# Rotating q and k in stacks of four tiles, scaling the attention probabilities on ScalarE, and a third w0 low part on GpSimd

## The chip, the cores and the metric

The kernel runs on one core of a Trainium2 chip. The core has five engines that work side by side, each on its own queue of instructions and in the order of that queue: TensorE (PE: matrix products, with weight loads called PEld in the profile), VectorE (DVE), ScalarE (ACT), GpSimd (POOL) and SyncE (SP, which issues most of the DMAs). They meet through semaphores. The metric is the device time of one execution in microseconds (us), here the median of the runs shown.

## The reference, cut to what matters

One layer of an encoder, float32 throughout, 512 positions of 1024 features. The part around the change is the attention branch: q and k are projected, the first 32 of the 128 features of each head are rotated by position, and three groups of four heads attend with a dilation of 1, 4 and 16. The groups are combined by weights from their softmax denominators.

```python
def partial_rope(t):                       # t: (B, S, H, 128)
    half = ROPE_DIM // 2                   # ROPE_DIM = 32
    ...
    x1, x2, rest = tf[..., :half], tf[..., half:ROPE_DIM], tf[..., ROPE_DIM:]
    return concatenate([x1 * cos - x2 * sin, x2 * cos + x1 * sin, rest], axis=-1)

def dilated_window_attention(q, k, v, dilation, radius):
    ...
    s = einsum('bdnqhe,bdnkhe->bdnhqk', qb, kw) * scale
    s = where(valid, s, MASK_VALUE)
    m = max(s, axis=-1, keepdims=True)
    p = exp(s - m)
    denom = sum(p, axis=-1, keepdims=True)
    o = einsum('bdnhqk,bdnkhe->bdnhqe', p, vw) / denom
    ...

def reference(x, ...):
    n = rms_norm(h, norm_mix_pre)
    z_gmlp, q, k, v, gates = split(n @ w_in, split_points)
    y_a = gmlp_spatial_gating(gelu(z_gmlp), ...)
    q, k = partial_rope(q), partial_rope(k)
    for g, (window, dilation) in enumerate(ATTN_PATTERNS):      # (128,1), (512,4), (2048,16)
        o_g, lse_g = dilated_window_attention(q[g], k[g], v[g], dilation, window // (2 * dilation))
    w_mix = softmax(stack(lses), axis=0)
    y_b = sum(w_mix[..., None] * stack(outs), axis=0)
    merged = sigmoid(gate_a) * (y_a @ w_branch_a) + sigmoid(gate_b) * (y_b @ w_branch_b)
    h = h + rms_norm(merged @ w_out, norm_mix_post)
    ...                                                         # and an MLP with relu squared
```

## The kernel before, in words

**Products.** Every large product is made of three matmuls in a one-pass float32 type (F32R): each operand is split into a high part (ScalarE copies it into F32R, `hi`) and a low part (a subtraction, `lo`, mostly on VectorE), and `mm3` (lines 82 to 86) adds high x high, high x low and low x high. So each weight tile of 128 x 1024 that TensorE uses is first split by one ScalarE and one VectorE instruction (`wsplit`, lines 70 to 76). In `nc.tensor.matmul(ps, a, b)` the first operand, a, is the stationary one that a weight load brings into the array, and b is the moving one that is streamed past it.

**The front.** The four blocks of x (in the order 1, 2, 3, 0) are loaded, squared and summed (`square_x`, ScalarE), scaled to `xn` on VectorE, turned by TensorE (line 180) into `pt`, and split into `nh` and `nl` (`norm_x`). Beside this the eight tiles of the first weight, w0, are split (`split_w0`); the low parts of tiles 3 and 7 are made by GpSimd, the other six by VectorE. For each block 24 matmuls give `pv`.

**The v groups 1 and 2** (`token_major`) take as stationary operand every fourth column of nh and nl: `n[:, k, ROT + r:ROT + S:4]`. A later product of the same form (`COL_V`) takes 128 neighbouring columns.

**The heads.** For each h of 4, `project_qk` goes through the groups g = 1, 2, 0; for each it loads the q and k weights, splits them and lets `feature_tile` make `pf` (24 matmuls of 128x512), the 128 features of the head by 512 positions. `rope_tile` then takes it out of PSUM:

```python
nc.vector.stream_shuffle(sw, ps[0:32], ...)                          # L312 swapped halves
nc.scalar.activation(dst, v(ps), AF.Copy)                            # L313
nc.gpsimd.tensor_tensor(sw, sw, rope[:, 1], op=ALU.mult)             # L314 times sin
nc.vector.tensor_tensor(dst[0:32], v(ps[0:32]), v(rope[:, 0]), ...)  # L315 times cos
nc.vector.tensor_tensor(dst[0:32], dst[0:32], v(sw), op=ALU.add)     # L316
```

For the groups 1 and 2, `v` reorders positions (l r) to (r l), so that `q1`, `k1`, `q2` and `k2` lie in SBUF as four runs of 128 neighbouring columns, one for each residue r. `scores_b` multiplies them in plain float32 (line 373, 32 matmuls of 128x128, each two records in the profile) into `psb`; `scores_a` does it for group 0 with split operands into `psa`. `softmax_tile` masks, takes the maximum (VectorE) and the exponential (ScalarE). `mix(h)` combines the groups: a short chain of small steps with two small matmuls, `pp` (line 398) and `pc` (line 421), and at its end VectorE scales the eight probability tiles (lines 427 and 429). `attend(h)` turns the scaled tiles on TensorE (lines 448, 461), splits or copies them (`ptah`, `ptal`, `ptb`) and multiplies with v into `py`; it is emitted while head h + 1 is projected. The attention of the last head is interleaved with the product `pf` of u that follows the product `pv` of `COL_V`.

**What sets the order.** The program is written once in Python; a scheduler then orders each engine's instructions by its own timing model, and the pools add waits wherever a tile's buffer is used again. Two pools matter here. In PSUM `psA`, tag "T" has a single buffer: `pp`, `pc`, the turned tiles `pt` of the heads 0 to 2 and the first `pf` of u take turns in it. Tag "acc" has four. In SBUF the weight halves `hi` and `lo` of `wpool` have three buffers each, so a new split waits until TensorE has used the one three before.

Of the kernel before, what the change touches and what calls it, by code (L numbers as in the profile page):

```python
# [16 lines left out]
P = 128  # L17
# [19 lines left out]
def block_kernel(ctx: ExitStack, tc: tile.TileContext, x, norm_mix_pre, w_in, b_gate, ln_v_gain, ln_v_bias,  # L37
# [151 lines left out]
    def split_w0(k):  # L189
        raw = w0raw[k // 2][:, k % 2]  # L190
        hi = w0pool.tile([P, GW], F32R, name="w0hi")
        lo = w0pool.tile([P, GW], F32R, name="w0lo")
        ins = nc.scalar.activation(hi, raw, AF.Copy)
        (nc.gpsimd if k in (3, 7) else nc.vector).tensor_tensor(lo, raw, hi.bitcast(F32), op=ALU.subtract)
        w0.append((hi, lo))
        return ins
# [111 lines left out]

    def rope_tile(ps, dst, perm):
        v = (lambda a: a.rearrange("p (l r) -> p r l", r=4)) if perm else (lambda a: a)  # L310
        sw = apool.tile([32, S], F32, name="sw", bufs=2)
        nc.vector.stream_shuffle(sw, ps[0:32], [(i + 16) % 32 for i in range(32)])  # L312
        nc.scalar.activation(dst, v(ps), AF.Copy)  # L313
        nc.gpsimd.tensor_tensor(sw, sw, rope[:, 1], op=ALU.mult)  # L314
        nc.vector.tensor_tensor(dst[0:32], v(ps[0:32]), v(rope[:, 0]), op=ALU.mult)  # L315
        nc.vector.tensor_tensor(dst[0:32], dst[0:32], v(sw), op=ALU.add)  # L316

    def project_qk(h):
        got = {}
        for g in (1, 2, 0):  # L320
            if g == 2 and h:
                attend(h - 1)
            hd0 = (g * NH + h) * HD
            raw = wload([2, KD, P], lambda r: [(r[:, 0], fcols(w_in, COL_Q + hd0, KD, P)), (r[:, 1], fcols(w_in, COL_K + hd0, KD, P))], "qkw")
            for j, nm in enumerate("qk"):
                wh, wl = wsplit(raw[:, j])
                ps = feature_tile(wh, wl, KD, nhn, nln)
                if g:
                    d = apool.tile([P, 4, P], F32, name=f"{nm}{g}")
                    rope_tile(ps, d, True)  # L330
                    got[nm, g] = d
                else:
                    t = apool.tile([P, S], F32, name="qk0t", bufs=2)
                    rope_tile(ps, t, False)
                    w = S if nm == "q" else S + P
                    o = 0 if nm == "q" else ROT
                    hi = apool.tile([P, w], F32R, name=f"{nm}0h")
                    lo = apool.tile([P, w], F32R, name=f"{nm}0l")
                    split_into(hi[:, o:o + S], lo[:, o:o + S], t)
                    if nm == "k":  # L340
                        for z, y in ((hi, nc.scalar), (lo, nc.vector)):
                            zf = z.bitcast(F32)
                            for dst, src in ((z[:, 0:ROT], zf[:, S:S + ROT]), (z[:, S + ROT:], zf[:, ROT:2 * ROT])):
                                if y is nc.scalar:
                                    y.activation(dst, src, AF.Copy)
                                else:
                                    y.tensor_copy(dst, src)
                    got[nm, g] = (hi, lo)
            if g == 2:
                scores_b(h, got)  # L350
        scores_a(h, got)

# [39 lines left out]
    def mix(h):  # L392
# [585 lines left out]
def _constants():  # L978
# [3 lines left out]
    cos, sin = np.cos(ang).astype(np.float32).T, np.sin(ang).astype(np.float32).T  # L982
    rope = np.stack([np.concatenate([cos, cos]), np.concatenate([-sin, sin])]).astype(np.float32)
    i = np.arange(P)[:, None]
# [26 lines left out]
```

## Time and profile before

| what | value |
|---|---|
| median of 3 runs | 814.27 us (813.33 to 814.29) |
| the profiled execution | 814.04 us, of which 812.3 us is the span from the first to the last instruction |
| PE busy | 801.9 us, 99% of the span |
| DVE busy | 546.8 us, 67% |
| ACT busy | 371.6 us, 46% |
| POOL busy | 85.4 us, 11% |
| span 88 to 243 us (the heads): busy | PE 155.00, DVE 132.75, ACT 65.44, POOL 41.89 of 155 us |
| span 243 to 290 us (v of the gating, u, last head): busy | PE 47.00, DVE 32.06, ACT 22.11, POOL 15.80 of 47 us |

How to read it: a row of a group names the line, the engine, the operation, output<-inputs, the shape, and after the bar the busy time and the mean duration of one. In a timeline the first number is the start in us from the span's start, the second the time covered; a remark in brackets says how long the engine was idle before it and for what. The durations of matmuls are modelled with their way through the array, so the pace of TensorE is read from the distances of starts, not from durations. In the waits, "A <- B" means that A's engine sat idle until B had ended.

### The profile page before, as it was taken

To read this page: it belongs to the slowest core of one execution; us is meant where nothing else is said; L and a number is where in the kernel's file an instruction comes from. 1 tells how busy PE (TensorE), PEld (TensorE's weight loads), DVE (VectorE), ACT (ScalarE), POOL (GpSimd) and SP (SyncE) were. 2 spreads that over 40 slices of the span, in tenths; PEclk is the share of its full clock that TensorE was granted. 3 is DMA by queue.
4 is the path that set the end of the run, shared out by engine and by line. 5 is a ranking of instruction groups with operands and counts; after the bars stand their busy time and mean duration, and the time that the engine had idled before them with its cause. 6 is when DMAs were issued, how large, how long until landed. Compare 5 with 4: busy or idle time off the path is not lost.

```text
span 812.3 us, 11650 instructions
## 1 busy us (share of the span) xinstructions
PE 801.9 (99%) x4629; PEld 711.8 (88%) x4629; DVE 546.8 (67%) x916; ACT 371.6 (46%) x609; POOL 85.4 (11%) x92
## 2 busy tenths in 40 slices
PE   8999999999999999999999999999999999999996
PEld 5899888888888889999988899999999888888885
DVE  6772788978783978788656579988887533333324
ACT  6342334434344545454535447666676522332212
POOL 2012113232222400000000200000000000000000
PEclk9999999999999999999999999999999999999999
DMA  9367333232131283244446223333334632332202
GB/s 294 123 228 187 98 104 104 53 90 67 52 104 53 65 284 105 79 112 122 130 137 227 103 79 94 114 105 104 106 108 144 235 109 103 104 104 77 79 1 104
DMA packets 83960, 95.34 MB, mean 117 GB/s; under 512 B 2417, under 2 KB 70033, under 8 KB 82882
## 3 DMA queue, kind: packets, MB, share of 16 engines
q1 hardware_dynamic: 80208, 77.60, 31.5%
q0 software_dynamic: 3696, 17.00, 6.0%
q8 instruction: 36, 0.59, 0.3%
q14 instruction: 18, 0.15, 0.1%
q10 hardware_dynamic: 2, 0.00, 0.0%
HBM read 86.20 MB, written 8.39 MB: 116 GB/s over the span
## 4 chain that ended last, share of the span: by engine, by line
PE 94%; DMA 2%; DVE 2%; ACT 1%; SPq 0%; issue 0%; DVEq 0%; POOLq 0%; ACTq 0%
PE pacc L880 12%; PE pd L85 9%; PE pd L84 9%; PE pd L86 9%; PE pf L86 9%; PE pf L85 9%; PE pf L84 9%; PE pgacc L555 6%; PE ptp L880 4%; PE pv L84 4%; PE pv L85 3%; PE pv L86 3%; PE pgS L555 2%; DMA xt<-in_x_dram 1%; PE psb L373 1%; PE py L485 1%
## 5 line engine op out<-in xcount | busy, mean ns | idle before, releaser
L84 PE MATMUL pf<-nh,hi 128*128 128x512 f32 x240 | 94.6, 394 | 0.0
L85 PE MATMUL pf<-nl,hi 128*128 128x512 f32 x240 | 94.5, 394 | 0.0
L86 PE MATMUL pf<-nh,lo 128*128 128x512 f32 x240 | 94.2, 392 | 0.0
L85 PE MATMUL pd<-hl,hh 128*128 128x512 f32 x224 | 87.2, 389 | 0.0
L84 PE MATMUL pd<-hl,hh 128*128 128x512 f32 x224 | 86.2, 389 | 0.0
L86 PE MATMUL pd<-hl 128*128 128x512 f32 x224 | 86.0, 389 | 0.0
L80 DVE TENSOR_TENSOR hl<-hid,hh 128x512 fp32r<-128x512 f32 x28 | 19.2, 693 | 75.6 <-ACT hh L79 75.6
L880 PE MATMUL pacc<-nt,hl 128*128 128x256 f32 x504 | 67.7, 280 | 0.1
L880 PEld LDWEIGHTS pacc<-nt,hl 128*128 128x128 f32 x504 | 62.7, 188 | 0.4 <-ACT hl L79 0.3
L79 ACT ACTIVATE hh<-hid 128x512 fp32r<-128x512 f32 x28 | 17.4, 630 | 89.0 <-PE pd L85 89.0
L314 POOL TENSOR_TENSOR sw<-sw,rope 32x512 f32<-32x512 f32 x24 | 41.9, 1745 | 131.7 <-DVE sw L312 114.6
L86 PEld LDWEIGHTS pf<-nh,lo 128*128 128x128 f32 x240 | 45.1, 188 | 8.9
L84 PEld LDWEIGHTS pf<-nh,hi 128*128 128x128 f32 x240 | 45.1, 188 | 8.7
L85 PEld LDWEIGHTS pf<-nl,hi 128*128 128x128 f32 x240 | 45.1, 188 | 8.6
L86 PEld LDWEIGHTS pd<-hl 128*128 128x128 f32 x224 | 42.0, 188 | 8.8
L84 PEld LDWEIGHTS pd<-hl,hh 128*128 128x128 f32 x224 | 42.0, 188 | 8.7
L85 PEld LDWEIGHTS pd<-hl,hh 128*128 128x128 f32 x224 | 42.0, 188 | 8.5
L80 DVE TENSOR_TENSOR hl<-dnw,hl 128x1024 fp32r<-128x1024 f32 x32 | 39.1, 1225 | 13.9 <-ACT hl L79 13.9
L74 ACT ACTIVATE hi<-qkw 128x1024 fp32r<-128x1024 f32 x24 | 25.4, 1058 | 49.3 <-PE pf L85 25.5
L880 PE MATMUL pacc<-n,hl 128*128 128x256 f32 x336 | 45.2, 280 | 0.4 <-ACT z L905 0.4
L75 DVE TENSOR_TENSOR lo<-qkw,hi 128x1024 fp32r<-128x1024 f32 x24 | 36.9, 1538 | 12.1 <-ACT hi L74 11.5
L79 ACT ACTIVATE hl<-s 128x1024 fp32r<-128x1024 f32 x28 | 29.6, 1058 | 29.1 <-DVE s L864 10.8
(317 smaller groups left out, 1992.3 us busy)
## 6 DMA issues: line engine op xcount, KB each, us to landing
upw<-in_w_up_dram SPq DMA_DIRECT2D x16, 1024.0 KB, 5.5
dnw<-in_w_down_dram SPq DMA_DIRECT2D x16, 1024.0 KB, 4.9
qkw<-in_w_in_dram SPq DMA_DIRECT2D x24, 512.0 KB, 5.3
gw<-in_w_in_dram SPq DMA_DIRECT2D x16, 512.0 KB, 5.4
slab<-in_w_in_dram SPq DMA_DIRECT2D x6, 1024.0 KB, 9.8
sum<-sum POOLq DMA_DIRECT2D x4, 1024.0 KB, 7.8
nt<-sum POOLq DMA_DIRECT2D x4, 1024.0 KB, 8.0
wow<-in_w_out_dram SPq DMA_DIRECT2D x4, 1024.0 KB, 4.8
```

Source lines behind the costliest of these rows:

```text
L74: nc.scalar.activation(hi, raw, AF.Copy)
L75: (sub or nc.vector).tensor_tensor(lo, raw, hi.bitcast(F32), op=ALU.subtract)
L79: nc.scalar.activation(hi, src, AF.Copy)
L80: return nc.vector.tensor_tensor(lo, src, hi.bitcast(F32), op=ALU.subtract)
L84: nc.tensor.matmul(ps, ah, bh, start=start, stop=False)
L85: nc.tensor.matmul(ps, ah, bl, start=False, stop=False)
L86: return nc.tensor.matmul(ps, al, bh, start=False, stop=stop)
L314: nc.gpsimd.tensor_tensor(sw, sw, rope[:, 1], op=ALU.mult)
L373: nc.tensor.matmul(ps[:, rr, g - 1], got["q", g][:, r], got["k", g][:, r], start=True, stop=True)
L485: nc.tensor.matmul(o, v12[:, g, r, hs], ptb[r // 2][:, r % 2, g], start=False, stop=(r == 3 and g == 1), skip_group_check=True)
L555: nc.tensor.matmul(ps, a[:, j], b[:, j], start=first and not (j or i), stop=(j == KH - 1 and i == 2), skip_group_check=True)
L880: nc.tensor.matmul(ps, a[:, j], b[:, j], start=first and not (j or m), stop=(j == KH - 1 and m == 2), skip_group_check=True)
```

## The change

1. In the front, the low part of w0 tile 5 is made by GpSimd too, and the squares of the third and fourth block are emitted after the high part of the second block, not before.
2. `rope_tile` is replaced. ScalarE copies each `pf` out in plain order (`d`) and its first 32 rows once more into 32 rows of a stack `st` of 128 partitions. When q1, k1, q2 and k2 are there, `rotate` shuffles, multiplies and adds the whole stack at once, and ScalarE copies the four results back into the first 32 rows of each tile. q0 and k0 are a second stack of 64 rows. The table `rope` has its 32 rows four times.
3. The reordering is gone from the copies: `got` holds a view, `d.rearrange("p (l r) -> p r l", r=4)`, so `scores_b` reads every fourth column.
4. The eight probability tiles are scaled by ScalarE.

```diff
-        (nc.gpsimd if k in (3, 7) else nc.vector).tensor_tensor(lo, raw, hi.bitcast(F32), op=ALU.subtract)
+        (nc.gpsimd if k in (3, 5, 7) else nc.vector).tensor_tensor(lo, raw, hi.bitcast(F32), op=ALU.subtract)
...
-        with tc.issue_after(ins.ins):
-            rs[2], sq = square_x(blocks[2], xts[2])
...
         if i == 0:
             with tc.issue_after(hi.ins):
-                rs[3], _ = square_x(blocks[3], xts[3])
+                for j in (2, 3):
+                    rs[j], _ = square_x(blocks[j], xts[j])
...
-    rope = apool.tile([32, 2, S], F32, name="rope")
+    rope = apool.tile([P, 2, S], F32, name="rope")
...
+    def rotate(st, tiles):
+        rows = 32 * len(tiles)
+        sw = apool.tile([P, S], F32, name="sw")
+        nc.vector.stream_shuffle(sw[:rows], st[:rows], [(i + 16) % 32 for i in range(32)])
+        nc.gpsimd.tensor_tensor(sw[:rows], sw[:rows], rope[:rows, 1], op=ALU.mult)
+        nc.vector.tensor_tensor(st[:rows], st[:rows], rope[:rows, 0], op=ALU.mult)
+        nc.vector.tensor_tensor(st[:rows], st[:rows], sw[:rows], op=ALU.add)
+        for i, d in enumerate(tiles):
+            nc.scalar.activation(d[0:32], st[32 * i:32 * i + 32], AF.Copy)
...
+            if g != 2:
+                st, tiles = apool.tile([P, S], F32, name="st", bufs=2), []
...
                 ps = feature_tile(wh, wl, KD, nhn, nln)
-                if g:
-                    d = apool.tile([P, 4, P], F32, name=f"{nm}{g}")
-                    rope_tile(ps, d, True)
-                    got[nm, g] = d
...
+                d = apool.tile([P, S], F32, name=f"{nm}{g}")
+                nc.scalar.activation(d, ps, AF.Copy)
+                i = len(tiles)
+                nc.scalar.activation(st[32 * i:32 * i + 32], ps[0:32], AF.Copy)
+                tiles.append(d)
+                got[nm, g] = d.rearrange("p (l r) -> p r l", r=4)
             if g == 2:
+                rotate(st, tiles)
                 scores_b(h, got)
+            elif g == 0:
+                rotate(st, tiles)
...
         for i in range(4):
-            nc.vector.tensor_scalar(probs[h, "b", i], probs[h, "b", i], cf[:, 1, i:i + 1], None, op0=ALU.mult)
+            nc.scalar.activation(probs[h, "b", i], probs[h, "b", i], AF.Copy, scale=cf[:, 1, i:i + 1])
         for i in range(4):
-            nc.vector.tensor_scalar(probs[h, "a", i], probs[h, "a", i], ca[:, i:i + 1], None, op0=ALU.mult)
+            nc.scalar.activation(probs[h, "a", i], probs[h, "a", i], AF.Copy, scale=ca[:, i:i + 1])
```

Lines of the changed kernel are a few numbers higher from `scores_b` on (the score matmul of line 373 stands on line 378, `pp` on 403, `pc` on 426).

The places where the scheduler's new order matters are shown next. First TensorE where the product `pv` of `COL_V` ends and the product `pf` of u begins, with the mix of the last head between them (`pp`, `pc`), in the program before:

```order
L398 MATMUL pp<-xa,perm 128x32
L85 MATMUL pv<-lo,nh 128x512
...
L84 MATMUL pv<-hi,nh 128x512
L85 MATMUL pv<-lo,nh 128x512
L421 MATMUL pc<-xc,perm 128x16
L86 MATMUL pv<-hi,nl 128x512
```

And in the changed program, the same place, with buffer numbers:

```order
L86 MATMUL pv_2210<-hi_2299,nl_80 128x512
L490 MATMUL py_1872<-ptb_1909,v12_89 128x128 x4
L403 MATMUL pp_2158<-xa_2156,perm_682 128x32
L426 MATMUL pc_2180<-xc_2178,perm_682 128x16
L84 MATMUL pf_2408<-nh_79,hi_2404 128x512
```

Before, 31 matmuls of `pv` stood between `pp` and `pc`; now all of `pv` stands ahead of `pp`, and `pc` and the first `pf` come right behind it.

VectorE in the changed program, from the result of `pp` to that of `pc`; `ybl` is the low part of head 2's output:

```order
L405 TENSOR_TENSOR xb_2160<-pp_2158,perm_682 128x32
L407 TENSOR_REDUCE mab_2162<-xb_2160 128x8
L409 TENSOR_TENSOR big_2164<-mab_2162,mdb_2003 128x4
L80 TENSOR_TENSOR ybl_383<-py_1872,ybh_382 128x512
L411 TENSOR_TENSOR e_2166<-mab_2162,big_2164 128x4
L412 TENSOR_TENSOR e_2166<-mdb_2003,big_2164 128x4
```

Before, `ybl` stood ahead of this chain; now it stands inside it.

ScalarE behind this, in the program before, from the square of the third `pv` tile on (`ptah` is the high part of the turned probabilities of the last head, `gt` the steps of gelu, `hi` a split of u's weights):

```order
L504 ACTIVATE gt_2379<-pv_2233 128x512
L504 ACTIVATE gt_2393<-pv_2234 128x512
L79 ACTIVATE ptah_2413<-pt_2408 128x512
L79 ACTIVATE ptah_2422<-pt_2417 128x512
L506 ACTIVATE gt_2379<-gt_2379 128x512
L506 ACTIVATE gt_2393<-gt_2393 128x512
```

And in the changed program, from the same square on:

```order
L509 ACTIVATE gt_2355<-pv_2209 128x512
L509 ACTIVATE gt_2369<-pv_2210 128x512
L74 ACTIVATE hi_2592<-uw_2545 128x1024
L511 ACTIVATE gt_2355<-gt_2355 128x512
L79 ACTIVATE ptah_2389<-pt_2384 128x512
L511 ACTIVATE gt_2369<-gt_2369 128x512
L79 ACTIVATE ptah_2398<-pt_2393 128x512
```

A weight split and a tanh now stand ahead of the first `ptah`.

More of the change, by code (lines that the diff above doesn't have):

```diff
@@ L307, in block_kernel @@
     by_c = perm[:, 2 * P + 4:2 * P + 8].unsqueeze(1).unsqueeze(3)
[L309 to L316, printed above, removed]
+    def rotate(st, tiles):
[7 more added lines that the diff above has]
+            nc.scalar.activation(d[0:32], st[32 * i:32 * i + 32], AF.Copy)
     def project_qk(h):
-        got = {}
+        got, tiles = {}, []
         for g in (1, 2, 0):
@@ L327, in project_qk @@
                 ps = feature_tile(wh, wl, KD, nhn, nln)
-                if g:
-                    d = apool.tile([P, 4, P], F32, name=f"{nm}{g}")
-                    rope_tile(ps, d, True)
-                    got[nm, g] = d
[L332 to L348, printed above, removed]
@@ L349, in project_qk @@
+                d = apool.tile([P, S], F32, name=f"{nm}{g}")
[4 more added lines that the diff above has]
+                got[nm, g] = d.rearrange("p (l r) -> p r l", r=4)
             if g == 2:
+                rotate(st, tiles)
                 scores_b(h, got)
+            elif g == 0:
+                rotate(st, tiles)
+        for nm, t in zip("qk", tiles):
+            w = S if nm == "q" else S + P
+            o = 0 if nm == "q" else ROT
+            hi = apool.tile([P, w], F32R, name=f"{nm}0h")
+            lo = apool.tile([P, w], F32R, name=f"{nm}0l")
+            split_into(hi[:, o:o + S], lo[:, o:o + S], t)
+            if nm == "k":
+                for z, y in ((hi, nc.scalar), (lo, nc.vector)):
+                    zf = z.bitcast(F32)
+                    for dst, src in ((z[:, 0:ROT], zf[:, S:S + ROT]), (z[:, S + ROT:], zf[:, ROT:2 * ROT])):
+                        if y is nc.scalar:
+                            y.activation(dst, src, AF.Copy)
+                        else:
+                            y.tensor_copy(dst, src)
+            got[nm, 0] = (hi, lo)
@@ L982, in _constants @@
     cos, sin = np.cos(ang).astype(np.float32).T, np.sin(ang).astype(np.float32).T
-    rope = np.stack([np.concatenate([cos, cos]), np.concatenate([-sin, sin])]).astype(np.float32)
+    rope = np.tile(np.stack([np.concatenate([cos, cos]), np.concatenate([-sin, sin])]).astype(np.float32), (1, 4, 1))
     i = np.arange(P)[:, None]
```

## The prediction

> **What bounds the kernel now.** I read the page first, then TensorE's busy time by stage, then the waits and timelines of the places that the change touches. The page's line of the engines, and the row of the stage of the heads from the table by stages (us, then busy us and instructions of PE, PEld, DVE, ACT, POOL, then the granted clock):
>
> ```profile
> PE 801.9 (99%) x4629; PEld 711.8 (88%) x4629; DVE 546.8 (67%) x916; ACT 371.6 (46%) x609; POOL 85.4 (11%) x92
> 88.00:243.00 155.00, 155.00 (x789) 131.50 (x788) 132.75 (x294) 65.44 (x132) 41.89 (x24) 1.00 0.29 82
> ```
>
> TensorE is busy in all 155 us of the heads, although VectorE works 132.75 us there. So what the change takes off VectorE is worth nothing by itself; what it adds to TensorE, or makes TensorE wait for, counts in full. Three places count: the front, the score matmuls, and the end of `pv`.
>
> **Part 1: reading every fourth column.** `scores_b` now gets q (stationary) and k (moving) with a step of four columns. The program before has one product with such a stationary operand, the v groups. Weight loads there (40 to 80 us), of the same line with neighbouring columns (250 to 265 us), and those of the scores today:
>
> ```profile
> L84 PEld LDWEIGHTS pv<-hi,nh 128*128 128x128 f32 x57 | 17.2, 310 | 0.0
> ...
> L84 PEld LDWEIGHTS pv<-hi,nh 128*128 128x128 f32 x20 | 3.8, 188 | 0.7
> ...
> L373 PEld LDWEIGHTS psb<-k,q x64: 187/192/193, 104.1 to 233.4; 128*128 128x128 f32 x64
> ```
>
> The same load takes 310 ns with the step and 188 ns without. What this does to the pace shows in TensorE's timeline, twelve matmuls from the first row to the second with the step, and twelve from the third to the fourth without; then a group of twelve score records, one `pf`, and the `pf` behind it:
>
> ```profile
> 57.17 0.40 PE L84 MATMUL pv<-hi,nh 128*128 128x512 f32 x1
> 59.99 0.40 PE L84 MATMUL pv<-hi,nh 128*128 128x512 f32 x1
> ...
> 88.00 0.39 PE L84 MATMUL pf<-nh,hi 128*128 128x512 f32 x1
> 90.72 0.39 PE L84 MATMUL pf<-nh,hi 128*128 128x512 f32 x1
> ...
> 112.50 1.50 PE L373 MATMUL psb<-k,q 128*128 128x128 f32 x12
> 114.08 0.39 PE L86 MATMUL pf<-nh,lo 128*128 128x512 f32 x1
> ```
>
> With the step a matmul starts every 2.82 / 12 = 0.235 us, without it every 2.72 / 12 = 0.227. A matmul of 512 columns hides a long load nearly whole, yet the pace became that of the load: one stepped load per 0.235 us. A score record streams only 128 columns and hides nothing: today one takes (1.58 - 0.227) / 12 = 0.113 us. With loads of 0.235 us each, 64 records cost 64 x (0.235 - 0.113) = **+7.9 us**. Lower end 0, if a plain float32 load differs from an F32R one; but both take about 190 ns without a step, so I take the row.
>
> The moving side has no row on TensorE. The nearest is VectorE, which reads `sw` with the same step for group 1 and 2 and without it for group 0:
>
> ```profile
> L316 DVE TENSOR_TENSOR q<-q,sw 32x512 f32<-32x512 f32 x8 | 8.6, 1071 | 1.2 <-POOL sw L314 0.9
> L316 DVE TENSOR_TENSOR qk0t<-qk0t,sw 32x512 f32<-32x512 f32 x8 | 5.4, 677 | 0.4
> ```
>
> A stepped read costs it (1071 - 677) / 512 = 0.77 ns per column more. So the moving k is likely to be slower as well. If each column is read once in a record, that lies beside the load of 0.235 us and costs nothing more; if a record reads its columns twice, it takes 0.47 us, and the sum is 64 x (0.470 - 0.113) = 22.9 us. I take the first and keep the second as a rival. [...]
>
> **Part 2: the stacks and the scaling on ScalarE.** Per head VectorE and GpSimd lose work and ScalarE gains six copies of 32 rows in, six back and eight scalings. I cost this at nothing, except in Part 3, because of the distances in the new order. From the last matmul of k2 to the first score that needs it stood 34 matmuls in head 0, now 47, so 47 x 0.227 = 10.7 us. The new chain is longer by the second copy and the four copies back. A copy, the shuffle and the product on GpSimd:
>
> ```profile
> L313 ACT ACTIVATE q<-pf 128x512 f32<-128x512 f32 x8 | 4.8, 596 | 0.2
> L312 DVE STREAM_SHUFFLE sw<-pf 32x512 f32<-32x512 f32 x24 | 17.5, 728 | 0.0
> L314 POOL TENSOR_TENSOR sw<-sw,rope 32x512 f32<-32x512 f32 x24 | 41.9, 1745 | 131.7 <-DVE sw L312 114.6 <-DVE k0l L347 5.1 <-DVE xc L419 4.4
> ```
>
> Six copies at 0.6, 0.73, 1.75 and a sum of 0.68 make 6.8 us, some 8 with handovers: 2 to 3 us are left. Without that cover each head would lose what is missing. Heads 1 to 3 keep 44 or more matmuls, and slower scores only widen the gap. The rope table is four times larger, 512 KB, and is first needed only when four tiles are stacked.
>
> **Part 3: the end of `pv`.** This is where the order rows in the section on the change bite. `pp`, `pc` and the first `pf` of u share one PSUM buffer, and now nothing stands between them. The steps today, from the three timelines:
>
> ```profile
> 256.28 0.30 PE L398 MATMUL pp<-xa,perm 128*128 128x32 f32 x2
> 263.58 0.29 PE L421 MATMUL pc<-xc,perm 128*128 128x16 f32 x2
> 265.19 0.39 PE L86 MATMUL pv<-hi,nl 128*128 128x512 f32 x1
> ...
> 255.51 0.69 DVE L80 TENSOR_TENSOR ybl<-py,ybh 128x512 fp32r<-128x512 f32 x1 [2.76 <-ACT ybh L79]
> 257.29 0.16 DVE L406 TENSOR_TENSOR e<-mab,big 128x4 f32<-128x4 f32 x1
> 258.68 0.18 DVE L419 TENSOR_TENSOR xc<-cf,perm 128x16 f32<-128x16 f32 x1
> 263.91 0.17 DVE L423 TENSOR_TENSOR xd<-pc,perm 128x16 f32<-128x16 f32 x1 [4.00 <-PE pc L421]
> ...
> 254.88 0.60 ACT L79 ACTIVATE ybh<-py 128x512 fp32r<-128x512 f32 x1 [0.51 <-PE py L485]
> 265.66 1.06 ACT L74 ACTIVATE hi<-uw 128x1024 fp32r<-128x1024 f32 x1 [0.83 <-PE pv L86]
> ```
>
> Let T be the start of the last `py` group, right behind the last `pv`. TensorE is through with `py` and `pp` at T+0.95. The chain `pp` to `e` alone is 257.29 - 256.28 = 1.01 us, but `ybl` now stands in it, and that waits on ScalarE: a split `hi` that cannot start before the last `pv` is done (265.66 - 265.19 = 0.47 after its start, so T+0.24), 1.06; `ybh`, 0.60; `ybl`, 0.69: `e` starts at about T+2.6. From `e` to `xc` 1.39, `xc` itself and the handover 0.2: `pc` at T+4.2. `xd` 0.33 later and 0.17 long: the first `pf` starts at T+4.75. TensorE has idled 4.75 - 0.95 - 0.14 = **3.6 us**; without `ybl` in the chain it would still be 2.9.
>
> The debt goes on. Call the restart R. ScalarE now scales, and the gelu of `pv`, whose banks the next tiles need, queues behind:
>
> ```profile
> L362 ACT ACTIVATE p<-p,nm 128x256 f32<-128x256 f32 x32 | 15.9, 498 | 6.3 <-DVE nm L361 6.1
> ...
> 266.63 1.14 ACT L506 ACTIVATE gt<-gt 128x512 f32<-128x512 f32 x2
> 270.13 1.09 ACT L79 ACTIVATE ptah<-pt 128x512 fp32r<-128x512 f32 x2 [0.94 <-PE pt L448]
> ...
> 269.68 0.67 DVE L505 SCALAR_TENSOR_TENSOR gt<-gt,pv 128x512 f32<-128x512 f32 x1
> 271.06 1.28 DVE L80 TENSOR_TENSOR ptal<-pt,ptah 128x512 fp32r<-128x512 f32 x2
> 273.01 0.54 DVE L534 TENSOR_SCALAR vln<-vln,mv,rs_out 128x512 f32<-128x512 f32 x1
> ...
> 271.22 0.57 POOL L96 TENSOR_TENSOR rs_out<-rs_in,neghalf 128x1 f32<-128x1 f32 x1 [2.00 <-DVE rs_in L90]
> ```
>
> A scaling is taken at 0.45, an exponential of the same size less its read-out. From R-0.8 ScalarE does four scalings (to R+1.0), two squares (2.1), four scalings (3.9) and the first tanh (4.5). Then VectorE does five passes of 0.64 (7.7), ScalarE the next tanh (8.3) and `ptah` (8.85). TensorE needs `ptah` after 23 `pf`, eight turns and some small ones, at about R+6.8: 2.0 us. Its next turn needs `ptal`, which is behind the second gt (8.35), the statistics (8.65), `rs_out` (9.2), `vln` and one more pass (10.4): ready at 11.0, 2.1 us more. Back-to-back instructions overlap by 0.05 to 0.1, ten of them on this path, so 4.1 becomes 3.6. Part 3 together **+7.2 us**. Bounds: 2.9, if the other engines are ahead of my walk after R, and 9.
>
> **Part 4: the front.** TensorE's rows, then ScalarE and GpSimd:
>
> ```profile
> 14.18 1.15 PE L180 MATMUL pt<-ident,xn 128*128 128x128 f32 x8
> 16.03 0.50 PE L85 MATMUL pv<-w0lo,nh 128*128 128x512 f32 x1 [0.70 <-DVE w0lo L194]
> 17.48 0.50 PE L84 MATMUL pv<-w0hi,nh 128*128 128x512 f32 x1 [0.49 <-ACT nh L182]
> ...
> 15.61 0.63 ACT L169 ACTIVATE junk<-xt 128x512 f32<-128x512 f32 x1 [1.53 <-DMA xt<-in_x_dram]
> ...
> 14.16 1.27 POOL L194 TENSOR_TENSOR w0lo<-w0raw,w0hi 128x512 fp32r<-128x512 f32 x1 [1.31 <-ACT w0hi L193]
> ```
>
> Between 14.18 and 17.48 lie eight turns (0.75) and three matmuls (0.7): 1.45 us of work in 3.3, so 1.85 is to be had. GpSimd's row shows that tile 7's high part was there at 14.16; tile 5's is two splits of some 0.55 earlier, so its low part can be ready 1.27 after 13.05, at 14.3, and `nh` no longer queues behind a square that waits for its DMA. What is late next: the squares of the third block come after `nh`, and ScalarE's copy of the first `pv` and VectorE's low part fall into the turns of that block; I take back 0.35. **-1.5 us**, between 0 and -2.
>
> **Rivals.** (a) *The moving operand pays twice*, Part 1: 814.0 + 22.9 + 7.2 - 1.5 = 842.6, 842.8 against the median. For it: the VectorE rows. Against: a record need not read a column twice. (b) *The step costs a float32 load nothing*: 827.8 - 7.9 = 819.9. (c) *The clock drops in the pause.* Matmuls of 512 columns began at half pace here:
>
> ```profile
> 10.38 0.63 PE L84 MATMUL pv<-w0hi,nh 128*128 128x512 f32 x1
> 10.80 0.63 PE L85 MATMUL pv<-w0lo,nh 128*128 128x512 f32 x1
> ```
>
> Here they are 0.42 apart, against 0.227 later. If a pause of 3.2 us brings this back for some 3 us, half of those are lost: +1.5, 829.3. [...] (d) *Not slower.* Mechanism: the front's 1.5 to 2 us are kept, and neither stepped loads nor the pause cost: 812.5. It decides only if Parts 1 and 3 together stay under 1.5 us, and Part 3 follows from TensorE's order and one shared buffer, so little speaks for it.
>
> **How the numbers follow.** Own time 814.04 + 7.9 + 7.2 - 1.5 = 827.6; the median of the runs is 0.2 above the profiled execution, so 827.8. Chances: this 0.60 (its own range 823 to 831, by Part 3's bounds), (a) 0.18, (b) 0.09, (c) 0.07, (d) 0.03, within 0.2% 0.03; 0.2% is 1.6 us, about what a measurement of this kernel can tell from no change. The range reaches from (b) to (a), 820 to 843, since leaving both out would leave out more than 2 in 10.
>
> **What would show it.** Right: weight loads of the scores near 310 ns and 0.235 us per record; a TensorE wait of 3 us or more at `pc` with `pf` behind it, and waits at `py` on `ptah` and at the turn on `ptal`; none in the heads. Wrong: score loads at 190 ns; records near 0.47 us; no idle time at `pc`; waits for the rotated tiles at the scores.

## The result and the profile after

The changed kernel takes 833.63 us (median of 4 runs, 831.64 to 835.74) against 814.28 (813.33 to 815.02) for the kernel before on the same chip: a ratio of 1.0239, with a 95% interval of 1.0209 to 1.0268. The forecast was 827.8, so the direction and most of the mechanism held, and 5.8 us are to be explained. The profiled execution took 831.64 us, the fastest of the four, with a span of 829.9 us against 812.3 before: 17.6 us more.

The engines' line of the page, the row of the granted clock in 40 slices, and the row of the heads in the table by stages:

```profile
PE 812.1 (98%) x4629; PEld 721.4 (87%) x4629; DVE 489.7 (59%) x819; ACT 411.0 (50%) x689; POOL 58.0 (7%) x77
...
PEclk9999999999999899999999999999999999999999
```

```profile
88.00:243.00 155.00, 155.00 (x747) 132.78 (x746) 69.49 (x191) 93.56 (x188) 12.10 (x7) 1.00 0.29 82
```

VectorE's load in the heads fell from 132.75 to 69.49 us, and ScalarE's rose from 65.44 to 93.56. TensorE is busy in all 155 us as before, but got through 747 records instead of 789: nothing waits there, the records take longer. The dent in the clock's row, in slice 14 (270 to 290 us), is new. The longest of TensorE's waits:

```profile
PE pc L426 <- DVE xc L424: 4.7, 1, 4.7
PE pt L466 <- DVE ptal L80: 2.6, 1, 2.6
...
PE py L483 <- ACT ptah L79: 0.3, 1, 0.3
```

These are the waits that the prediction named, at the places that it named, in other sizes. The score matmuls, first their weight loads (min/median/max in ns), then TensorE's timeline from the start of a group of twelve to the second `pf` behind it:

```profile
L378 PEld LDWEIGHTS psb<-k,q x64: 308/330/333, 113.8 to 242.4; 128*128 128x128 f32 x64
```

```profile
115.24 2.95 PE L378 MATMUL psb<-k,q 128*128 128x128 f32 x12
...
118.27 0.40 PE L85 MATMUL pf<-nl,hi 128*128 128x512 f32 x1
```

A record takes (3.03 - 0.227) / 12 = 0.234 us, where it took 0.113: 64 x 0.121 = 7.7 us. The end of `pv`, from TensorE's timeline:

```profile
271.01 1.05 PE L490 MATMUL py<-ptb,v 128*128 128x128 f32 x8
271.89 0.31 PE L403 MATMUL pp<-xa,perm 128*128 128x32 f32 x2
276.87 0.61 PE L426 MATMUL pc<-xc,perm 128*128 128x16 f32 x2 [4.67 <-DVE xc L424]
277.74 0.79 PE L84 MATMUL pf<-nh,hi 128*128 128x512 f32 x1 [0.27 <-DVE xd L428]
278.34 0.63 PE L85 MATMUL pf<-nl,hi 128*128 128x512 f32 x1
...
284.96 1.03 PE L453 MATMUL pt<-ident,p 128*128 128x128 f32 x8
...
290.36 0.63 PE L466 MATMUL pt<-ident,p 128*128 128x128 f32 x4 [2.64 <-DVE ptal L80]
```

Two things in it were not in the sum. The pause is 4.67 + 0.27 us, not 3.6. And the 23 `pf` between 277.74 and 284.96 take 7.22 us instead of 23 x 0.227 = 5.22. The second has its row in the granted clock (the last column but two):

```profile
272.00:276.00 4.00, 0.20 (x3) 0.09 (x1) 3.42 (x8) 1.00 (x3) 3.04 (x3) 0.86 0.21 51
276.00:278.00 2.00, 0.86 (x3) 0.76 (x4) 1.05 (x8) 1.28 (x4) 0.00 (x0) 0.50 0.48 125
278.00:280.00 2.00, 2.00 (x5) 1.56 (x6) 1.07 (x2) 2.00 (x6) 0.00 (x0) 0.50 0.00 0
280.00:282.00 2.00, 2.00 (x7) 1.53 (x6) 0.69 (x2) 2.00 (x5) 0.00 (x0) 0.57 0.00 0
```

A mean of 0.86 over 4 us is 1.1 us at half, and one of 0.57 over 2 us is 1.7, so the clock is at half for 1.1 + 2 + 2 + 1.7 = 6.8 us, most of it while TensorE is working again. For the length of the pause, VectorE and GpSimd in the same microseconds, and again at the wait for `ptal`:

```profile
272.71 2.04 DVE L409 TENSOR_TENSOR big<-mab,mdb 128x4 f32<-128x4 f32 x1
...
286.55 2.46 DVE L539 TENSOR_SCALAR vln<-vln,mv,rs_out 128x512 f32<-128x512 f32 x1
```

```profile
272.39 2.34 POOL L75 TENSOR_TENSOR lo<-uw,hi 128x1024 fp32r<-128x1024 f32 x1 [4.47 <-ACT hi L74]
...
286.38 2.35 POOL L75 TENSOR_TENSOR lo<-uw,hi 128x1024 fp32r<-128x1024 f32 x1 [0.33 <-ACT hi L74]
```

`big` works on four columns and takes 2.04 us; in the kernel before it took 0.16. The `vln` takes 2.46 us, where others of its line take 0.53. Both began after the GpSimd pass beside them and end with it or just behind it: the passes end at 272.39 + 2.34 = 274.73 and 286.38 + 2.35 = 288.73, `big` at 274.75, `vln` at 289.01.

### The profile page after: what moved, and what is told of

It is laid out like the page before. It is cut to its first block, busy times and chain, and to the rows that moved or that the text cites. A ratio compares the mean times of both kernels' runs of the same rounds, so it can differ in the third digit from the quotient of the medians.

```text
span 829.9 us, 11578 instructions
## 1 busy us (share of the span) xinstructions
PE 812.1 (98%) x4629; PEld 721.4 (87%) x4629; DVE 489.7 (59%) x819; ACT 411.0 (50%) x689; POOL 58.0 (7%) x77
## 4 chain that ended last, share of the span: by engine, by line
PE 93%; DVE 4%; DMA 2%; ACT 1%; issue 0%; SPq 0%; DVEq 0%; POOLq 0%; ACTq 0%
PE pacc L885 11%; PE pd L84 9%; PE pd L86 9%; PE pd L85 9%; PE pf L84 8%; PE pf L85 8%; PE pf L86 8%; PE pgacc L560 6%; PE ptp L885 4%; PE pv L85 3%; PE pv L86 3%; PE pv L84 3%; PE pgS L560 2%; PE psb L378 2%; DMA w0raw<-in_w_in_dram 1%; PE py L490 1%
## 5 line engine op out<-in xcount | busy, mean ns | idle before, releaser
L75 DVE TENSOR_TENSOR lo<-qkw,hi 128x1024 fp32r<-128x1024 f32 x24 | 29.4, 1226 | 55.4 <-ACT hi L74 53.9
L885 PEld LDWEIGHTS pacc<-n,hl 128*128 128x128 f32 x336 | 41.9, 188 | 0.6 <-ACT z L910 0.6
```

The lines of the kernel that those rows point to most:

```text
L75: (sub or nc.vector).tensor_tensor(lo, raw, hi.bitcast(F32), op=ALU.subtract)
L885: nc.tensor.matmul(ps, a[:, j], b[:, j], start=first and not (j or m), stop=(j == KH - 1 and m == 2), skip_group_check=True)
```

## The experiments

All times are medians; the kernel before had 813.4, 813.8 and 813.8 us on the chips of the three groups of runs (scores and front; the next four; the last four), so the changed kernel corresponds to about 833 there.

**The scores: which operand pays.** Three kernels differ from the changed one only in how q and k are copied. The edit, here for both operands; the others do it for q or for k alone:

```
-                nc.scalar.activation(d, ps, AF.Copy)
+                nc.scalar.activation(d, turned(ps) if g else ps, AF.Copy)
...
-                got[nm, g] = d.rearrange("p (l r) -> p r l", r=4)
+                got[nm, g] = d.rearrange("p (r l) -> p r l", r=4)
...
-            nc.scalar.activation(d[0:32], st[32 * i:32 * i + 32], AF.Copy)
+            nc.scalar.activation(d[0:32], turned(st[32 * i:32 * i + 32]), AF.Copy)
```

Both contiguous:

> The changed kernel, but q and k of groups 1 and 2 are copied out of PSUM in permuted order (and the rotated rows copied back in it), so both operands of the score matmuls have neighbouring columns again; TensorE's order and all else are as in the changed kernel. Theory (a stepped float32 stationary operand costs TensorE 0.235 us a record): loads of the scores near 190 ns, 0.113 us a record, 64 x 0.121 = 7.7 us less than the changed kernel's 833.6, so about 825.9; the pause at pc stays. Rival (the step is free, the time was lost elsewhere): within 1.5 us of 833.6.

Measured: 825.93 us (823.88 to 826.75, ratio to before 1.0139, 1.0116 to 1.0161), as expected. Loads and pace are those of the kernel before, (1.57 - 0.227) / 12 = 0.112 us:

```profile
L383 PEld LDWEIGHTS psb<-k,q x64: 188/192/193, 113.2 to 234.1; 128*128 128x128 f32 x64
```

```profile
114.13 1.50 PE L383 MATMUL psb<-k,q 128*128 128x128 f32 x12
...
115.70 0.39 PE L85 MATMUL pf<-nl,hi 128*128 128x512 f32 x1
```

Only q contiguous, then only k:

> As the kernel with both operands contiguous, but only the stationary q is; k, the moving operand, keeps its step of four columns. Theory (the stationary side pays, the moving side nothing): loads near 190 ns, 0.113 us a record, about 825.9. Rival 1 (the moving side pays too, and was hidden behind the load): loads near 190 ns, but still 0.23 us a record or more, 833 or above. Rival 2 (in between): 0.15 to 0.2 us a record.

> The other half: the stationary q keeps its step of four columns, the moving k is contiguous. Theory (the stationary side pays): loads of 310 to 330 ns and 0.234 us a record as in the changed kernel, about 833.6. Rival (the moving side pays): 0.113 us a record, about 826.

Measured: 835.18 us (two runs) with k alone stepped, 831.87 (two runs) with q alone stepped. The first, loads and then twelve records:

```profile
L383 PEld LDWEIGHTS psb<-k,q x64: 187/208/209, 113.7 to 241.8; 128*128 128x128 f32 x64
```

```profile
115.09 2.88 PE L383 MATMUL psb<-k,q 128*128 128x128 f32 x12
...
118.04 0.40 PE L85 MATMUL pf<-nl,hi 128*128 128x512 f32 x1
```

The second:

```profile
L383 PEld LDWEIGHTS psb<-k,q x64: 308/329/332, 113.9 to 241.6; 128*128 128x128 f32 x64
```

```profile
115.17 2.84 PE L383 MATMUL psb<-k,q 128*128 128x128 f32 x12
...
118.08 0.39 PE L85 MATMUL pf<-nl,hi 128*128 128x512 f32 x1
```

With k alone stepped the loads are short again (208 ns), and a record still takes (2.95 - 0.227) / 12 = 0.227 us; with q alone stepped it takes (2.91 - 0.227) / 12 = 0.224. So the expectation for the first fell, and its rival 1 holds: the moving side pays as much as the stationary one. Either step costs 0.11 us a record, and both together 0.12: the two prices lie beside each other and don't add. To take one away gains next to nothing. This agrees with the prediction's choice that a moving column is paid for once (0.227 us a record, where paying twice was put at 0.47).

The 3.3 us between the two times are not the scores' (64 x 0.003 = 0.2 us). In the first kernel's profiled execution (834.85 us) the clock falls a second time, in the wait for `ptal`; in the second's (830.89) it does not:

```profile
288.00:290.00 2.00, 0.02 (x1) 0.05 (x1) 2.00 (x4) 1.00 (x2) 1.04 (x2) 0.61 0.00 0
```

From `ptr` to the first `pgacc`, the next products behind this wait, the first takes 42.5 us and the second 40.0. The mean clock is 0.991 in both runs of the first and 0.995 in both of the second.

**The front alone.** The kernel before with the front's three edits of the diff and nothing else.

> The kernel before with the front's part of the change alone: sixth low part on GpSimd and the square of the third block behind the high part of the second. Theory (the front gains what the changed kernel's trace shows there, where the turns of the fourth block stand 0.91 us earlier, and nothing behind gives it back): about 813.4, 0.9 below the kernel before. My predicted size of 1.5 would be 812.8. Rival (a later wait takes it back): 814.3.

Measured: 813.24 us (12 runs) against 813.4, ratio 0.9993, 0.9985 to 1.0002: no difference that the times can show. The first `pf` in the trace of before, then in that of this kernel (in the changed kernel's it starts at 81.65 us):

```profile
82.55 0.40 PE L84 MATMUL pf<-nh,hi 128*128 128x512 f32 x1
```

```profile
81.74 0.40 PE L84 MATMUL pf<-nh,hi 128*128 128x512 f32 x1
```

The front gains 0.9 us in the changed kernel and 0.8 alone, and that 0.8 is still there at the first `pacc` (491.23 us, 492.04 in before). Its profiled execution then lost 0.9 us between 492 and 637 us, spread over many matmuls without a wait; it was the slowest of the twelve (814.17). That loss is not the front's: the last section has it in traces of other kernels too. A gain of 0.8 lies inside the interval, and so does none.

**The pause: the shared bank.** `pp` and `pc` get buffers of another tag:

```
-        pp = psA.tile(shape, F32, name="pp", tag="T")
+        pp = psA.tile(shape, F32, name="pp", tag="S", bufs=2)
...
-        pc = psA.tile(sq, F32, name="pc", tag="T")
+        pc = psA.tile(sq, F32, name="pc", tag="S", bufs=2)
```

> The changed kernel with pp and pc in a PSUM bank of the pair S instead of the one that the first pf of u takes; TensorE's order then has 17 pv behind the last py group and 11 pf ahead of the last pc. Theory (the pause comes from the shared bank, and the dropped clock from the pause): no idle time at pc, the 24 pf at 0.227 us and a granted clock of 1.0 there; of the 10.7 us that the changed kernel lost from pc on, the 4.7 + 0.3 of idle time, 0.4 at half pace in pc and 2.0 in the pf go, and 2.6 to 4.5 of waits for ptah and ptal stay: 826 to 828. Rival (the softmax of the last head ends last whatever TensorE does meanwhile): the idle time moves whole to ptah, 5 us or more there, 831 or above.

Measured: 824.34 us (824.1 to 825.0, ratio 1.0128, 1.0113 to 1.0143), better than expected. In the microseconds of the softmax TensorE is now busy throughout, at full clock:

```profile
264.00:272.00 8.00, 8.00 (x42) 6.77 (x41) 3.75 (x13) 2.55 (x5) 2.38 (x1) 1.00 0.20 57
272.00:276.00 4.00, 4.00 (x20) 3.35 (x19) 1.19 (x4) 3.57 (x8) 2.06 (x1) 1.00 0.59 151
```

`big` is still slow there (1.56 us beside a GpSimd pass), and it costs nothing, because no matmul waits for it. Of the waits behind, 1.0 us is left at the second turn and 0.4 at `pg`. One edit of a buffer's tag takes away about 9 us of the changed kernel's loss.

**The clock: a filled pause.** Twenty products that nobody reads, in the pause:

```
         ins = nc.tensor.matmul(pp, perm[:, 0:P], xa, start=True, stop=True)
+        if h == NH - 1:
+            idle = psA.tile([P, S], F32, name="idle", tag="S", bufs=2)
+            for k in range(20):
+                with tc.issue_after(ins.ins):
+                    ins = nc.tensor.matmul(idle, nhn[:, k % KD, 0:P], nhn[:, k % KD], start=True, stop=True)
```

> The changed kernel with 20 products of 512 columns, whose result nobody reads, between the last pp and pc (4.5 us of the pause; the output is the reference's). Theory (the clock falls because TensorE idles, but the work behind is set by ScalarE and VectorE, which started from pc all the same): the pf run at 0.227 us from the first on, granted clock 1.0, and the 2.0 us so won are waited for at ptah (2.3 us instead of 0.34), so pp to prs stays near the 19.65 us of the changed kernel's trace and the time within 1.5 us of 833.6. Rival (the dropped clock sets the end, as in rival (c) of the prediction): pp to prs 17.6 us, 831.6 or less. Rival 2 (the slow pf had another cause than the idle time): the pf stay at 0.43 us at first.

Measured: 828.98 us (828.89 to 830.06). More work on TensorE made the kernel some 4 us faster: the expectation fell, and its rival, the prediction's rival (c), holds. The `pf` run at full pace from the first on (granted clock 1.00 from 272 to 290 us):

```profile
272.18 4.83 PE L408 MATMUL idle<-nh 128*128 128x512 f32 x20
...
277.73 0.50 PE L84 MATMUL pf<-nh,hi 128*128 128x512 f32 x1 [0.27 <-DVE xd L433]
...
283.31 1.03 PE L458 MATMUL pt<-ident,p 128*128 128x128 f32 x8
```

The turns start 283.31 - 277.73 = 5.58 us after the first `pf` (with 24 `pf` ahead; 7.22 with 23 in the changed kernel), and the time won is not waited for at `ptah`: in the changed kernel ScalarE had been waiting for TensorE's `pf` there (its row at 285.22, a `hi`, has 1.77 us of idle time behind `pf`), not the other way round. Beside it, the new order on VectorE has `ptal` ahead of the `vln` that is slow in the changed kernel, and the wait there is 0.9 instead of 2.6 us. This part is not the clock's, so its price is read from the starts and not from the 4 us.

**`big` beside GpSimd's pass.** The first try:

> The changed kernel, but GpSimd's low part of the second u slab (128x1024, 2.34 us), which ran beside the softmax of the last head, is held back until xc; TensorE's order is the same. Theory (VectorE's big, two operands in SBUF, took 2.04 us instead of 0.16 because that pass held it up): big at 0.16 us, the wait at pc 4.67 - 1.9 = 2.8 us; the clock may then stay up, 2.0 us more; what TensorE gains it loses in part to a longer wait for ptah, so the changed kernel's 833.6 falls by 1.9 to 4, 830 to 832. Rival (big is slow for another reason, such as its wait for ScalarE): big stays near 2 us, the wait near 4.7, and the time within 1 us of 833.6.

Measured: 834.02 us (832.97 to 834.88). The edit held nothing back: the second low part of u starts at 265.56 us, as in the changed kernel (265.54) and 11 us ahead of `xc`. The one beside `big` is the third in any case. So the order on the engines stayed what it was, `big` at 2.04 us included. The run says nothing on the question, and stands as a repeat of the changed kernel. The second try ties the third low part to `xc` by data:

```
+        if behind is not None:
+            nc.gpsimd.tensor_tensor(lo[:, 0, 0:4], behind[:, 0, 0], behind[:, 0, 0], op=ALU.subtract)
         (sub or nc.vector).tensor_tensor(lo, raw, hi.bitcast(F32), op=ALU.subtract)
...
-            wh, wl = wsplit(raw[:, :, j * P:(j + 1) * P], sub=nc.gpsimd)
+            wh, wl = wsplit(raw[:, :, j * P:(j + 1) * P], sub=nc.gpsimd, behind=mixed[NH - 1] if g == 2 else None)
```

> The changed kernel with GpSimd's low part of the third u slab (2.34 us, the one that ran beside big) made to read four columns of xc first, so that it cannot start before xc; the order on TensorE, VectorE and ScalarE is the same. Theory (that pass held up big): big at 0.16 us instead of 2.04, the wait at pc 2.8 instead of 4.67; 1.9 less than the changed kernel's 833.6 to 834.0, and 2.0 more if so short a pause leaves the clock up: 830 to 832. Rival (big is slow for another reason): big stays at 2 us and the time within 1 us of 834.

Measured: 833.36 us (832.36 to 834.36). `big` and the first `vln`, GpSimd's third low part, and TensorE's wait at `pc`:

```profile
272.64 0.16 DVE L412 TENSOR_TENSOR big<-mab,mdb 128x4 f32<-128x4 f32 x1
...
284.19 2.56 DVE L543 TENSOR_SCALAR vln<-vln,mv,rs_out 128x512 f32<-128x512 f32 x1
```

```profile
275.34 2.40 POOL L77 TENSOR_TENSOR lo<-uw,hi 128x1024 fp32r<-128x1024 f32 x1
```

```profile
PE pc L430 <- DVE xc L428: 2.8, 1, 2.8
```

That the pass holds `big` up is settled: with it away, the same instruction takes 0.16 us and the wait at `pc` is 2.84. The time was to fall by 1.9 and did not, within the spread. The trace says where it went: the turns start 2.4 us earlier than in the changed kernel (282.61 against 284.96), but in the wait for `ptal` the clock falls again, for 6.8 us (its rows are in the last section), which in the changed kernel's profiled execution it did not. What the traces show beside a GpSimd pass of 1024 columns: `big`, which reads two tiles in SBUF, took 2.04 us in the changed kernel and 1.56 with the other bank, against 0.16 here; the `tensor_scalar` on `vln` took 2.46 us in the changed kernel and 2.56 here, against 0.53 without a pass; a `ptal`, with one input in PSUM, took its usual 0.68 us (in the filled kernel, at 285.62 us). By what the pass holds the one up and not the other, no run shows.

The fourth low part was held back in the same way until the first `vln`:

> As the kernel whose third low part waits for xc, and the fourth low part of u made to read four columns of the first normalised vln first, so that it cannot run beside that vln (2.46 us in the changed kernel's profile, 0.53 where GpSimd is idle). Theory (the wait for ptal is to 1.9 us the same kind of hold-up): vln at 0.54 us, the wait for ptal 0.7 or less, no second drop of the clock: 1.9 or more below the kernel with the third low part alone held back, 828 to 830. Rival (ptal waits for the rest of the chain): within 0.7 us of that kernel.

Measured: 830.4 us (828.71 to 831.75). VectorE:

```profile
284.30 0.55 DVE L543 TENSOR_SCALAR vln<-vln,mv,rs_out 128x512 f32<-128x512 f32 x1
...
285.36 2.70 DVE L543 TENSOR_SCALAR vln<-vln,mv,rs_out 128x512 f32<-128x512 f32 x1
```

The first `vln` is free, at 0.55 us, and now the second runs beside the pass and takes 2.70: the block moved by one instruction. TensorE waits 1.1 us for `wst` in a new order instead of 2.7 for `ptal`. The clock fell a second time here too (granted 0.67 in 286 to 288 us and 0.50 in 288 to 290), which the expectation had excluded. The time fell by 3 us, to just above the expected range, but only the first `vln` shows the reason that was given.

**The scaling back on VectorE.** Its two lines of the diff undone, the rest as in the changed kernel.

> The changed kernel with the probabilities scaled by VectorE again; in TensorE's order pp, pc and the pf of u still follow each other with nothing between. Theory (ScalarE's scalings do not make the pause, they only delay what follows it): idle time at pc 4 to 5 us as before and the dropped clock too; ScalarE is free 3.4 us earlier, VectorE has 8 x 0.41 = 3.3 us more, so the waits for ptah and ptal together change by less than 1.5 us: 832 to 834.5. Rival (the scalings on ScalarE are the cause of the tail's loss): pause and waits go, 826 or less.

Measured: 830.06 us (829.76 to 830.8). The pause at `pc` is 4.7 us as before and the clock falls (the `pf` from 278.59 to 284.14 us start 0.43 us apart), so ScalarE's scalings do not make the pause: that half holds. The time is 2 us below the expected range: the waits for `ptah` and `ptal` are gone. VectorE scales in 0.285 us (four in 1.14 us), not 0.41, and with ScalarE's split of the next weights later, GpSimd's pass begins at 288.53, behind the first two `vln`, which take 0.54 and 0.53 us.

**The sums.** Contiguous q and k with the other bank, and then the scaling on VectorE as well:

> Contiguous q and k and the bank of the pair S for pp and pc, both edits in one kernel; stacks, scaling on ScalarE and the front are as in the changed kernel. Theory (the two losses are independent): 824.3 of the kernel with the other bank less 7.7 for the scores = 816.6. Rival (faster scores bring the softmax no earlier and a wait takes some back): 818 to 820.

> Contiguous q and k, the other bank for pp and pc, and the probabilities scaled by VectorE again: what is left of the change is the stacks of four tiles and the front. Theory (the stacks cost nothing in the heads, the front keeps its 0.8 us up to the second half): within 1.6 us of the kernel before, 812.5 to 815.5. Rival (the longer way of the rotated rows, two copies more per tile and the sixteen copies back, costs TensorE something in each head): 816 or more.

Measured: 816.79 us (10 runs, ratio 1.003, 1.0018 to 1.0042), as expected, so the two losses add up; and 816.93 (10 runs, ratio 1.0035, 1.0023 to 1.0046), 1.4 above the expected range. The heads of the last kernel and two of TensorE's waits:

```profile
88.00:243.00 155.00, 155.00 (x788) 131.50 (x788) 82.48 (x229) 96.68 (x175) 12.51 (x8) 1.00 0.29 82
```

```profile
PE pg L617 <- DVE vln L544: 0.9, 1, 0.9
...
PE pt L471 <- DVE ptal L80: 0.6, 1, 0.6
```

Its rival is wrong too: in the heads TensorE is busy throughout and gets through 788 records, one less than before. Behind the front, which gains 0.8 us, the span loses 3.2 us (814.7 in all against 812.3), and 2.7 of these are in these two waits and two more of 0.6 us (at the turn of `wsp` and at a `pf`), in the last head's attention and the gelu, which the kernel before does not have. No version of the change beats the kernel before by more than can be measured; the front alone comes nearest.

## Why the prediction was right, and where it fell short

The sum against the profiled executions (us). The pause and the waits are measured as the prediction counted them, from start to start, less the work between:

| Term | Predicted | Measured |
|---|---|---|
| front | -1.5 | -0.9 |
| scores | +7.9 | +7.7 |
| pause, `pp` to first `pf` | +3.6 | +5.6 (4.94 of it idle time) |
| waits for `ptah` and `ptal` | +3.6 (2.0 and 2.1, less overlap) | +3.4 (idle time 0.34 and 2.64) |
| clock, in the 23 `pf` | 0 | +2.0 |
| rest, not tied to a row | | -0.2 |
| sum | 13.6 | 17.6 |

The pause is 6.73 - 0.95 - 0.14 us in the prediction's terms. The two waiting instructions of TensorE start 1.00 and 3.02 us behind the one ahead of each, where the same two took 0.41 and 0.20 before.

- **Part 1** was right in size. Its reason was half of the truth: the price is not that of the load alone, since the moving operand alone gives the same pace (0.227 us). The rival (a), 0.47 us, is out: 0.234.
- **Part 2** was right: no wait in the heads. The cover of 2 to 3 us held: in head 0 the last copy back ends at 111.66 us and the first score starts at 114.08.
- **Part 3** had the place and the chain right and took the durations of two steps, `big` and `vln`, from the kernel before, where no GpSimd pass held them up. The walk had the first `pf` at T+4.75, T being the start of the last `py` group. It came at T+6.73 (277.74 - 271.01), and in the kernel with the third low part held back at T+4.69 (275.63 - 270.94). So the walk to the first `pf` was right but for one step: `big` took 1.88 us longer, nearly all of the difference. The wait for `ptah` was too long in the walk: the other engines were ahead of it, which the prediction had as its lower bound. The wait for `ptal` came out near its 2.1 by chance: the walk had five passes of VectorE, the trace one blocked `vln`, 1.9 us longer than alone.
- **Part 4**: -0.9 instead of -1.5, inside its bounds. The term that was mis-sized is the 1.85 us to be had: the turns of the third block start only 1.05 us earlier than before (22.92 us against 23.97). Those of the fourth start 0.91 earlier, so 0.14 is taken back between them, where the sum had 0.35 for what is late next. Part of the missing 0.8 is the same hold-up as at `big`. VectorE's low part of a w0 tile, which reads two tiles in SBUF, runs beside GpSimd's two (merged in one row):

```profile
13.05 2.54 POOL L194 TENSOR_TENSOR w0lo<-w0raw,w0hi 128x512 fp32r<-128x512 f32 x2 [0.26 <-ACT w0hi L193]
...
14.41 1.73 DVE L194 TENSOR_TENSOR w0lo<-w0raw,w0hi 128x512 fp32r<-128x512 f32 x1
```

  It takes 1.73 us, the others of its line 0.69, and TensorE waits 0.33 us for it. The trace before had the sign of this at the same place: beside the GpSimd row that Part 4 shows at 14.16, a low part of VectorE took 1.50 us, and it was the one that TensorE's row at 16.03 waited for.
- **Rival (c)** came true beside the forecast and not in its place. It was sized at 1.5 us for one drop of 3 us; the drop lasted 6.8 us and cost 2.0. The front, from which it was sized, had its slow pace from 8.93 to 12.08 us at a granted clock of 1.00, so no run shows that pace to be the clock's; what the runs show is the 0.50 behind the pause. It was wrong to hold it at 0.07 as a case of its own: it came with the pause (with the pause filled, or gone with the other bank, the granted clock stays at 1.00), and whoever forecasts the pause should have asked the clock's price with it.
- **The range.** The measured 833.6 lies above the forecast's own range of 823 to 831, mainly by the two prices that the sum left out, the blocked `big` and the clock. That the full range of 820 to 843 holds it is owed to rival (a), which the runs refuted: that part is luck.

These terms explain 831.6, the profiled execution and the fastest of the four. For the 2.0 us up to the median there is one trace: the first try of the section on `big`, a repeat of the changed kernel, took 833.98 us in its profiled execution. Its `ptr` starts 0.65 us earlier than the changed kernel's, since the clock's first drop lasted 3.4 us and not 6.8. But the clock fell a second time, at 290.7 us, and from `ptr` to the first `pgacc` it took 41.9 us, the changed kernel 40.0. Another 1.1 us were lost behind 510 us at full clock; the last section has them in traces with and without the change. The kernel with contiguous q and k has the same order and waits (4.7, 2.6), and in its profiled execution the clock fell a second time too:

```profile
282.00:284.00 2.00, 1.44 (x7) 1.47 (x8) 2.00 (x4) 0.76 (x2) 0.00 (x0) 0.50 0.00 0
```

From `ptr` to the first `pgacc` it took 42.8 us there: 2.8 us for a drop that one execution has and another has not. In the changed kernel the runs' mean clocks go with their times: 0.995 and 0.994 in the runs of 831.64 and 832.73, 0.991 and 0.989 in those of 835.74 and 834.53. In the repeat they do not (0.995 in the runs of 833.98 and 834.06, 0.991 in that of 832.97). The kernels whose clock stays up (the other bank, the filled pause) spread by 1.2 us or less. That the second drop is in the slower runs of the changed kernel itself is argued from this; none of them has a trace.

## What to carry to other kernels

When an edit changes what stands between two instructions of a small serial chain, look first at which PSUM buffer the next large work needs: one shared bank cost about 9 us, a pause of 5 us (1.9 of them from a pass on another engine), the clock that fell in it, and longer waits behind it. Price a pause of TensorE with the half clock behind it (here 6.8 us at half, 2.0 us lost, behind 4.94 us of idle time), and price each link of a chain beside whatever GpSimd will be running then, not at the duration it had elsewhere (`big` took 2.04 us instead of 0.16). And the step of four columns in these matmuls of 128 columns was paid by the stationary and by the moving side (0.224 and 0.227 us a record for one alone, 0.112 without), so only both together can be undone with profit.

## What the runs showed of the hardware that was not expected

- The drops of the clock that were measured lasted 3.4 us or twice that. In the kernel with the third low part held back it was at half for 0.9 + 2 + 0.52 = 3.4 us, in the changed kernel for 6.8, twice that. In the first of the two it then stood at full for 6.8 us (280.5 to 287.4) and at half for 6.8 again (to 294.2):

```profile
277.00:278.00 1.00, 1.00 (x5) 0.76 (x4) 0.96 (x2) 1.00 (x4) 1.00 (x2) 0.55 0.00 0
278.00:280.00 2.00, 2.00 (x6) 1.61 (x5) 0.69 (x2) 2.00 (x5) 0.43 (x2) 0.50 0.32 98
280.00:281.00 1.00, 1.00 (x4) 0.73 (x4) 1.00 (x3) 0.77 (x3) 0.00 (x0) 0.74 0.18 66
...
286.00:288.00 2.00, 0.00 (x0) 0.00 (x0) 2.00 (x4) 1.02 (x2) 1.16 (x2) 0.84 0.00 0
...
294.00:296.00 2.00, 2.00 (x10) 1.58 (x10) 2.00 (x7) 0.00 (x0) 0.86 (x2) 0.96 0.00 0
```

  The first drop began at about 277.1 us, 1.5 us behind the first `pf`, after an idle time of 2.84 us. A wait of 2.6 us lowers the clock in one trace and not in another: at the wait for `ptal` it fell in the kernel with contiguous q and k (idle for 2.64 us, granted 0.50 from 282 to 288 us) and stayed at 1.00 in the changed kernel (also 2.64). What decides this, no run shows.
- The stage of `pacc`, behind 490 us, takes one of two times in the 14 traces of this case, 140.5 to 140.7 us (7 traces) or 141.6 (7), from its first start to its last. The clock is at full in both. The kernel before, then the one with the front alone:

```profile
L880 PE MATMUL pacc<-nt,hl x504: 276/280/384, 492.0 to 632.7; 128*128 128x256 f32 x168
```

```profile
L879 PE MATMUL pacc<-nt,hl x504: 276/280/385, 491.2 to 632.8; 128*128 128x256 f32 x168
```

  The cause stays open. Two single traces can differ by 0.9 us for this alone.
- A stationary step alone and a moving step alone give nearly the same pace (0.224 and 0.227 us for 128 columns, 0.112 without), though the load's own record grows far more with the first (329 ns) than with the second (208; 192 without a step).
